# Down-projection of a gated MLP: form before activation at its start, parked transfers one step later, two output rows in its third phase

## The chip, the cores and the metric

The program runs on one core of one Trainium2 chip. The metric is the time of one execution on the device in microseconds (us), the median of several runs. In the profile the engines are PE (TensorE, matmuls), PEld (its weight loads), DVE (VectorE), ACT (ScalarE), POOL (GpSimd) and SP (SyncE, which here only issues DMAs). ACTq and SPq are the instruction queues of ACT and SP; a DMA issued from one stands in it in order with everything else that the engine is given.

## The reference

One layer of a decoder: a conditioned first half (recurrence and sparse attention) and a conditioned gated MLP. The change touches only the second half of the MLP. T = 512 tokens, D = 1024, F = 2816, all f32:

```
h2 = rmsnorm(x, norm2_g) * (1.0 + sc2) + sh2
u = causal_dwconv(h2 @ w_up, conv_w, conv_b)     # 512 x 5632, three taps over the tokens
a, v = split(u, 2, axis=-1)
x = x + gt2 * ((silu(a) * v) @ w_down)           # 512 x 2816 by 2816 x 1024
```

## The kernel before

**Arithmetic.** Each f32 operand is split into a rounded part and a remainder, both in the format fp32r: `split` (L143, L144) casts on ACT (`whi<-raw`) and subtracts on DVE (`wlo<-raw,whi`). Every product is then three matmuls (`mm3`, L147 to L149). In what follows a *form* is such a pair of split weights; `form` puts two of three forms into the buffers `whi`/`wlo` (two of each) and the third into the single buffer `w3`, which the profile shows as `w`. So form k+3 reuses the buffer of form k and its cast has to wait until the matmuls of form k are done.

**Up-projection.** 44 steps `st`, one of 128 columns each; f = st // 2 counts the 22 pairs of gate (s = 0) and value (s = 1). Step st multiplies (`up_mm`, PE tile `u`), and two steps later `up_post` (L1597) makes the convolution of it: an ACT operation (L1603), two on DVE (L1604, L1605), then Silu on ACT for a gate (L1608), and for a value the product with the gate (L1610).

**Down-projection.** It is one level of a seven-product scheme of 2 by 2 blocks: tokens in halves of 256, columns of `w_down` in halves of 512, rows of `w_down` by even and odd f. With two values f of a pair j at hand, `g_parts` (L1627) makes the sums of activations that the seven products need (`s12`, `s34`) and splits them (`gP`, `gQ`, `st22`, `st34`). These are small jobs in a list `work`; each `up_post` starts with `step(3)` (L1621), which issues the next three. The last job of a pair is `park` (L1653): two DMAs on ACT's queue that write `st22` and `st34` to HBM (`pk`), from which they come back later as `S` and `A`.

The products are walked in phases of twelve steps, and a step is one form against the stationary activations of one or two pairs j: 12 matmuls of 512 columns for two pairs, 6 for one. `ORDERS` gives the steps (q, e), q = 0 to 5 a group of weight rows, e one of the phase's two products. The first phase does products 1 and 5 (from `gP`), the second 6 and 2 (from `gQ`), the third 7 and 3 (from `S`), and a last stage does product 4 (from `A`). The weights arrive in four sets, `da`, `db`, `dx` and `dy`, six loads each. In `forms` (L1681) DVE makes weight sums (`sum_a` L1667, `sum_b` L1673 and L1674, `sum_c` L1678) and then the form. `look()` takes the next form from it, three steps ahead.

**Order around the change.** `phase` (L1792) does for each step: the product; if the group q is new, `each(q)`; after step (5, 0) `done()`, which combines accumulators; then `look()`. In the first phase `each(0)` is `up_post` of the last value column, so the last activation work stands ahead of the form for step 3 on ACT and DVE. The gate before it, st = 42, is finished by `up_post` before the phase, with its Silu.

The accumulators are four pairs of PSUM banks (PE and DVE tile `dn`): `bS` is complete after the second phase (first two row tiles, first half of the columns), `bV` after the third (first two row tiles, second half), `bW` after `end_c` near the end of the third phase (last two row tiles, second half), and `bR` at the very end. `dn_out` (L1738 to L1743) multiplies by the gate row `gt2`, adds the residual (`rest`, 512 KB for each row tile, loaded by `load_rest` from `x1d`) and issues the DMA out on SP. In the last stage the loop at L1849 does four steps, each followed by one `dn_out` (`bV[0]`, `bV[1]`, `bW[0]`, `bW[1]`), then L1861 and L1862 scale `bR` and add the residual, and three closing pieces (512, 256 and 256 columns) are multiplied, added on DVE (L1867) and sent out on SP (L1868).

**Queues.** All loads stand in SP's queue in the order in which the program issues them. A load waits there until its tile's buffer is free, and each DMA, of SP or of ACT, takes the next of eight completion semaphores and waits until the DMA that used it eight places before has landed. One that waits holds up all that stands behind it.

Of the kernel before, what the change touches and what calls it, by code (L numbers as in the profile page):

```python
# [102 lines left out]
def hybrid_layer_kernel(ctx: ExitStack, tc: tile.TileContext, d: dict, out: bass.AP, dbg=None):  # L103
# [526 lines left out]
    def each(f):  # L630
        while True:
            f()
            yield
# [960 lines left out]
            mm3(us[st][:, sl], hi[:, k], lo[:, k], h2T[k // 2][0][:, k % 2, sl], h2T[k // 2][1][:, k % 2, sl], k == 0,  # L1594
                k == KT - 1)

    def up_post(st):  # L1597
        f, s = divmod(st, 2)
        u = us.pop(st)
        step(3)  # L1600
        c = s * NFF + f
        y = TMP([P, T], tag="y")
        sc.activation(y, u, AF.Identity, bias=cv[:, 132 + c:133 + c], scale=cv[:, 88 + c:89 + c])  # L1603
        ve.scalar_tensor_tensor(y[:, 1:], u[:, :T - 1], cv[:, 44 + c:45 + c], y[:, 1:], ALU.mult, ALU.add)  # L1604
        ve.scalar_tensor_tensor(y[:, 2:], u[:, :T - 2], cv[:, c:c + 1], y[:, 2:], ALU.mult, ALU.add)  # L1605
        ys[s] = y
        if s == 0:
            sc.activation(y, y, AF.Silu)  # L1608
        else:
            ve.tensor_tensor(ys[0], ys[0], y, ALU.mult)  # L1610
            g_parts(f, ys[0])

# [14 lines left out]
    def g_parts(f, y):  # L1627

        j, odd = divmod(f, 2)
        tt = ve.tensor_tensor  # L1630
        if not odd:
            gP[j] = G([2, 2, 256], F32R, s="gP")
            s4 = G([4, 256], s="s4")
            work.extend([(split, gP[j][:, 0, 0], gP[j][:, 0, 1], y[:, h1]),
                         (tt, s4[:, 2], y[:, h1], y[:, h2], ALU.subtract)])
            evens[0] = y, s4
            return
        e, s4 = evens.pop(0)
        s12, s34 = s4[:, 0:2], s4[:, 2:4]
        gQ[j] = G([2, 2, 256], F32R, s="gQ")  # L1640
        st22 = TMP([P, 2, 256], F32R, tag="st22")
        st34 = G([2, 2, 256], F32R, s="st34")
        work.extend([(tt, s12[:, 0], e[:, h2], y[:, h2], ALU.add),
                     (tt, s12[:, 1], s12[:, 0], e[:, h1], ALU.subtract),
                     (tt, s34[:, 1], y[:, h1], s12[:, 1], ALU.subtract),
                     (split, gQ[j][:, 0, 0], gQ[j][:, 0, 1], y[:, h1]),
                     (split, st22[:, 0], st22[:, 1], y[:, h2]),
                     (split, gP[j][:, 1, 0], gP[j][:, 1, 1], s12[:, 0]),
                     (split, gQ[j][:, 1, 0], gQ[j][:, 1, 1], s12[:, 1]),
                     (split, st34[:, 0], st34[:, 1], s34),  # L1650
                     (park, j, st22, st34)])

    def park(j, st22, st34):  # L1653
# [63 lines left out]
    def product(bank, n, q, w, start=False, rows=False):  # L1717

        hi, lo = w
        bs = range(min(2, NJ - 2 * q))  # L1720
        for a, b in [(a, b) for a in range(2) for b in bs] if rows else [(a, b) for b in bs for a in range(2)]:
            mm3(bank[a], *stat(n, 2 * q + b, a), hi[:, b], lo[:, b], start and q + b == 0, False)
# [63 lines left out]


    look()
    up_post(nst - 2)
    bR, bW, bS, bV = ([PS("dn") for _ in range(2)] for _ in range(4))  # L1790

    def phase(n, xb, x, yb, y, done, each):  # L1792
        seen = set()
        for q, e in ORDERS[n > 0]:
            w = ready.pop(0)
            product((xb, yb)[e], (x, y)[e], q, w, n == 0)
            if q not in seen:
                seen.add(q)
                each(q)
            if (q, e) == (NQ - 1, 0):  # L1800
                if n < 2:
                    sums_first()
                done()
            look()

    def end_a():
        for a in range(2):
# [7 lines left out]
        for a in range(2):  # L1815
            ve.tensor_tensor(bW[a], bR[a], w5[a], ALU.add)

    def each_a(q):
        if q == 0:
            up_post(nst - 1)  # L1820
        else:
            step(3)
            load_s34(q - 1)

    def each_b(q):
        load_s34(q + NQ - 1)

    def gate(q):
        ve.tensor_tensor(keep[q], keep[q], gt2[:, 0:512].unsqueeze(1).to_broadcast(list(keep[q].shape)), ALU.mult)

    def each_c(q):
        if q in (1, 2):
            load_rest()
        if q in (2, 3):
            gate(q + 2)
        if q in (3, 4):
            dn_out(bS[q - 3], q - 3, 0)
        load_a22(q)

    phase(0, bR, 1, bW, 5, end_a, each_a)  # L1840
    w5 = [TMP([P, T], tag="w5") for _ in range(2)]
# [1 line left out]
        sc.copy(w5[a], bW[a])  # L1843
    phase(1, bR, 6, bS, 2, end_b, each_b)
    phase(2, bR, 7, bV, 3, end_c, each_c)
    outs = [(bV[0], 0, 1), (bV[1], 1, 1), (bW[0], 2, 1), (bW[1], 3, 1)]
    lead = slice(0, 512)
    ws = []
    for q in range(NQ):  # L1849
        w = ready.pop(0)  # L1850
        if q < 2:
            load_rest()
        if q < NQ - 2:
            product(bR, 4, q, w, rows=q == NQ - 3)
            look()
            dn_out(*outs[q])
        else:
            ws += [(hi[:, b], lo[:, b], 2 * q + b) for hi, lo in [w] for b in range(min(2, NJ - 2 * q))]
    for a in range(2):
# [3 lines left out]
    for bank, a, cols in ((bS[0], 0, lead), (bS[1], 1, slice(0, 256)), (bV[0], 1, slice(256, 512))):  # L1863
        for n, (hi, lo, j) in enumerate(ws):
            mm3(bank[:, cols], *stat(4, j, a), hi[:, cols], lo[:, cols], n == 0, n == len(ws) - 1)
        t = rest[2 + a][:, cols]
        ve.tensor_tensor(t, bank[:, cols], t, ALU.add)  # L1867
        sp.dma_start(out_view[:, 2 + a, cols], t)  # L1868


_INS = ["x", "c", "positions", "w_ada", "b_ada", "norm1_g", "w_in", "lb_logits", "hg_norm_g", "q_norm_g",
# [18 lines left out]
```

## Time and profile before

| | |
|---|---|
| median of 3 runs | 691.7 us (691.69 to 692.68) |
| the profiled execution | 691.81 us, of which the span from first to last instruction is 690.0 us |
| mean granted TensorE clock | 0.997 |
| PE, DVE, ACT busy | 98%, 81%, 52% of the span |
| up-projection ends, first phase begins | 574.5 us |
| second phase, third phase, last stage begin | 610.0, 639.9, 669.9 us |
| last matmul starts | 684.90 us |

Rows of the timeline give start, duration, engine, line, operation, tiles written and read, and in brackets how long the engine had idled and what released it. A matmul's duration overlaps the next matmul, so the distance between two starts says what one costs. Rows of windows give the window and its length, then busy time (and count) of PE, PEld, DVE, ACT and POOL, the granted PE clock, the share of the 16 DMA engines and GB/s.

### The profile page before, as it was taken

To read this page: it belongs to the slowest core of one execution; us is meant where nothing else is said; L and a number is where in the kernel's file an instruction comes from. 1 tells how busy PE (TensorE), PEld (TensorE's weight loads), DVE (VectorE), ACT (ScalarE), POOL (GpSimd) and SP (SyncE) were. 2 spreads that over 40 slices of the span, in tenths; PEclk is the share of its full clock that TensorE was granted. 3 is DMA by queue.
4 is the path that set the end of the run, shared out by engine and by line. 5 is a ranking of instruction groups with operands and counts; after the bars stand their busy time and mean duration, and the time that the engine had idled before them with its cause. 6 is when DMAs were issued, how large, how long until landed. Compare 5 with 4: busy or idle time off the path is not lost.

```text
span 690.0 us, 10199 instructions
## 1 busy us (share of the span) xinstructions
PE 675.7 (98%) x3749; PEld 560.1 (81%) x3749; DVE 558.9 (81%) x1080; ACT 357.9 (52%) x688; POOL 56.3 (8%) x69
## 2 busy tenths in 40 slices
PE   8999999999999999999999999999999998999997
PEld 4678898687988889888988888888888886888886
DVE  5698988999889898687767787787878777888886
ACT  5564447565577669344554445444545445453431
POOL 1007153403000000200100000000000000000000
PEclk9999999999999999999999999999999999999999
DMA  9996544486123133443353745636634455869943
GB/s 280 291 313 204 151 154 152 142 256 184 32 93 123 32 95 123 151 135 119 119 153 91 200 135 171 185 104 192 197 115 115 120 183 177 298 226 374 367 138 122
DMA packets 107447, 117.48 MB, mean 170 GB/s; under 512 B 6731, under 2 KB 84355, under 8 KB 107397
## 3 DMA queue, kind: packets, MB, share of 16 engines
q1 hardware_dynamic: 103397, 105.98, 49.5%
q10 hardware_dynamic: 4000, 10.86, 4.1%
q8 instruction: 29, 0.48, 0.3%
q14 instruction: 21, 0.17, 0.1%
HBM read 103.96 MB, written 12.85 MB: 169 GB/s over the span
## 4 chain that ended last, share of the span: by engine, by line
PE 74%; DVE 14%; DMA 4%; SPq 3%; ACT 2%; issue 2%; ACTq 0%; POOL 0%; DVEq 0%; POOLq 0%
PE u L147 11%; PE u L148 11%; PE u L149 11%; PE dn L148 4%; PE dn L149 4%; PE dn L147 4%; PE oT L1068 2%; SPq L300 2%; PE F L1040 2%; PE pT L147 2%; PE pT L149 2%; PE pT L148 2%; DVE wlo L144 2%; PE oh L149 2%; PE oh L147 2%; PE oh L148 2%
## 5 line engine op out<-in xcount | busy, mean ns | idle before, releaser
L144 DVE TENSOR_TENSOR wlo<-raw,whi 128x1024 fp32r<-128x1024 f32 (+1 forms) x58 | 70.0, 1207 | 31.7 <-ACT whi L143 31.4
L147 PE MATMUL u<-h2h,whi 128*128 128x512 f32 (+1 forms) x248 | 93.3, 376 | 0.0
L148 PE MATMUL u<-h2l,whi 128*128 128x512 f32 (+1 forms) x248 | 93.1, 375 | 0.0
L149 PE MATMUL u<-h2h,wlo 128*128 128x512 f32 (+1 forms) x248 | 93.1, 375 | 0.0
L143 ACT CAST whi<-raw 128x1024 fp32r<-128x1024 f32 (+1 forms) x58 | 59.2, 1020 | 50.3 <-PE u L148 28.2
L148 PEld LDWEIGHTS u<-h2l,whi 128*128 128x128 f32 x248 | 46.7, 188 | 8.4
L149 PEld LDWEIGHTS u<-h2h,wlo 128*128 128x128 f32 x248 | 46.7, 188 | 8.4
L147 PEld LDWEIGHTS u<-h2h,whi 128*128 128x128 f32 x248 | 46.7, 188 | 8.3
L147 PE MATMUL u<-h2h,w 128*128 128x512 f32 (+1 forms) x128 | 48.1, 376 | 0.0
L148 PE MATMUL u<-h2l,w 128*128 128x512 f32 (+1 forms) x128 | 48.1, 376 | 0.0
L149 PE MATMUL u<-h2h,w 128*128 128x512 f32 (+1 forms) x128 | 48.1, 376 | 0.0
L1008 ACT ACTIVATE pt<-pt,mx 128x128 f32<-128x128 f32 (+3 forms) x64 | 35.8, 561 | 20.7 <-DVE mx L992 20.4
L1603 ACT ACTIVATE y<-u,cv 128x512 f32<-128x512 f32 x44 | 34.1, 775 | 19.4 <-DVE st L144 19.4
L1608 ACT ACTIVATE y<-y 128x512 f32<-128x512 f32 x22 | 13.9, 633 | 56.6 <-DVE y L1605 56.5
L1604 DVE SCALAR_TENSOR_TENSOR y<-u,cv,y 128x511 f32<-128x511 f32 x44 | 32.8, 745 | 12.2 <-ACT y L1603 12.2
L147 PE MATMUL pT<-hT,whi 128*128 128x512 f32 x96 | 38.7, 403 | 0.0
L149 PE MATMUL pT<-hT,wlo 128*128 128x512 f32 x96 | 37.6, 392 | 0.0
L148 PE MATMUL pT<-hT,whi 128*128 128x512 f32 x96 | 37.5, 391 | 0.0
L1605 DVE SCALAR_TENSOR_TENSOR y<-u,cv,y 128x510 f32<-128x510 f32 x44 | 32.9, 748 | 1.5
L1047 ACT COPY pT<-F 128x512 f32<-128x512 f32 (+2 forms) x52 | 25.8, 498 | 12.8 <-PE F L1040 12.4
L992 DVE CUSTOM_DVE_ANT_0 pt<-S,cmask 128x128 f32<-128x128 f32 (+3 forms) x64 | 29.6, 482 | 3.1 <-PE S L987 3.1
L376 POOL TENSOR_TENSOR hrs<-hrs,mhalf 128x4 f32<-128x4 f32 (+2 forms) x16 | 20.2, 1269 | 136.8 <-DVE hrs L375 136.7
(411 smaller groups left out, 1751.0 us busy)
## 6 DMA issues: line engine op xcount, KB each, us to landing
raw<-in_w_up SPq DMA_DIRECT2D x44, 512.0 KB, 5.1
ada<-in_w_ada SPq DMA_DIRECT2D x48, 256.0 KB, 5.2
aw<-in_w_ada SPq DMA_DIRECT2D x24, 512.0 KB, 4.5
raw<-in_w_down SPq DMA_DIRECT2D x10, 1024.0 KB, 4.8
raw<-in_w_in SPq DMA_DIRECT2D x7, 1024.0 KB, 6.2
rawd<-in_w_down SPq DMA_DIRECT2D x12, 512.0 KB, 9.2
pk<-st ACTq DMA_DIRECT2D x11, 512.0 KB, 2.6
S<-pk SPq DMA_DIRECT2D x11, 512.0 KB, 8.3
```

The costliest lines, as they stand in the source:

```text
L143: sc.copy(hi, src)
L144: (eng or ve).tensor_tensor(lo, src, f32(hi), ALU.subtract)
L147: pe.matmul(o, ah, bh, start=start, stop=False, skip_group_check=True)
L148: pe.matmul(o, ah, bl, start=False, stop=False, skip_group_check=True)
L149: pe.matmul(o, al, bh, start=False, stop=stop, skip_group_check=True)
L376: gp.tensor_tensor(o, o, mhalf[:, 0:n], ALU.pow)
L992: ve.tensor_tensor_reduce(pt[:, sl], ps[:, sl], cmask[:, 512 - W:512], -1.0, 1e30, ALU.add, ALU.min, mx[:, e:e + 1])
L1008: sc.activation(pt[:, sl], pt[:, sl], AF.Exp, bias=mx[:, e:e + 1], scale=-1.0, accum_out=su[:, h % 2, e:e + 1])
L1047: sc.copy(pT, ps[:, 0:n * P])
L1603: sc.activation(y, u, AF.Identity, bias=cv[:, 132 + c:133 + c], scale=cv[:, 88 + c:89 + c])
L1604: ve.scalar_tensor_tensor(y[:, 1:], u[:, :T - 1], cv[:, 44 + c:45 + c], y[:, 1:], ALU.mult, ALU.add)
L1605: ve.scalar_tensor_tensor(y[:, 2:], u[:, :T - 2], cv[:, c:c + 1], y[:, 2:], ALU.mult, ALU.add)
```

## The change

It has four parts, all around the down-projection.

1. **`phase` and its callbacks.** A step is now product, `done()`, `look()`, and then `each(k)` with the number of the step. In the first phase `up_post(42)` no longer issues the Silu of the last gate; that stands behind the form for step 3 (`each_a(0)`), and `up_post(43)` stands behind the form for step 4 (`each_a(1)`). The other `step(3)` calls and the loads of `S` move to odd and even steps.
2. **Parking.** An empty job is put ahead of `park`, which so becomes the first job of the next `step(3)`, one `up_post` later.
3. **Third phase.** All four `load_rest` stand in its first four steps, before it was two there and two in the last stage. The outputs of `bS` stand one step earlier, and those of `bW` after its last two steps instead of in the last stage. The last stage keeps the outputs of `bV`.
4. **The second closing piece** goes out on ACT's queue instead of SP's.

No arithmetic is added or removed. The diff:

```
-    def up_post(st):
+    def up_post(st, silu=True):
...
-        if s == 0:
+        if s == 0 and silu:
             sc.activation(y, y, AF.Silu)
-        else:
+        if s:
             ve.tensor_tensor(ys[0], ys[0], y, ALU.mult)
             g_parts(f, ys[0])
...
                      (split, st34[:, 0], st34[:, 1], s34),
+                     (lambda: None,),
                      (park, j, st22, st34)])
...
-    up_post(nst - 2)
+    up_post(nst - 2, False)
...
     def phase(n, xb, x, yb, y, done, each):
-        seen = set()
-        for q, e in ORDERS[n > 0]:
-            w = ready.pop(0)
-            product((xb, yb)[e], (x, y)[e], q, w, n == 0)
-            if q not in seen:
-                seen.add(q)
-                each(q)
+        for k, (q, e) in enumerate(ORDERS[n > 0]):
+            product((xb, yb)[e], (x, y)[e], q, ready.pop(0), n == 0)
             if (q, e) == (NQ - 1, 0):
...
                 done()
             look()
+            each(k)
...
-    def each_a(q):
-        if q == 0:
+    def each_a(k):
+        if k == 0:
+            sc.activation(ys[0], ys[0], AF.Silu)
+        elif k == 1:
             up_post(nst - 1)
+        elif k % 2:
+            step(3)
         else:
-            step(3)
-            load_s34(q - 1)
+            load_s34(k // 2 - 1)
-    def each_b(q):
-        load_s34(q + NQ - 1)
+    def each_b(k):
+        if k % 2:
+            load_s34(k // 2 + NQ - 1)
...
-    def each_c(q):
-        if q in (1, 2):
+    def each_c(k):
+        if k in (0, 1, 2, 3):
             load_rest()
-        if q in (2, 3):
-            gate(q + 2)
-        if q in (3, 4):
-            dn_out(bS[q - 3], q - 3, 0)
-        load_a22(q)
+        if k in (4, 6):
+            gate(k // 2 + 2)
+        if k in (5, 7):
+            dn_out(bS[k // 2 - 2], k // 2 - 2, 0)
+        if k % 2 == 0:
+            load_a22(k // 2)
+        if k > 9:
+            dn_out(bW[k - 10], k - 8, 1)
...
-    outs = [(bV[0], 0, 1), (bV[1], 1, 1), (bW[0], 2, 1), (bW[1], 3, 1)]
...
-        if q < 2:
-            load_rest()
         if q < NQ - 2:
             product(bR, 4, q, w, rows=q == NQ - 3)
             look()
-            dn_out(*outs[q])
+            if q < 2:
+                dn_out(bV[q], q, 1)
...
-        sp.dma_start(out_view[:, 2 + a, cols], t)
+        (sc if cols.start == 0 and a else sp).dma_start(out_view[:, 2 + a, cols], t)
```

**Place one, the start of the first phase, on ACT.** Numbers in the names tell buffers apart: `u_5703` is the last gate column, `u_5744` the last value column, `keep_5788` holds the weight sum for step 3 and `raw_5786` the weights for step 4. Before:

```order
L143 CAST st_1002_5702<-s_991_5621 128x512
L1654 DMA pk_3608<-st_1001_5701 128x512
L1655 DMA pk_3607<-st_1002_5702 128x1024
L1603 ACTIVATE y_5799<-u_5703,cv 128x512
L1608 ACTIVATE y_5799<-y_5799 128x512
L143 CAST gP_5784<-y_5739 128x256
L1603 ACTIVATE y_5827<-u_5744,cv 128x512
L143 CAST whi_5835<-keep_5788 128x1024
L143 CAST whi_5855<-raw_5786 128x1024
```

Now:

```order
L143 CAST st_1002_5702<-s_991_5621 128x512
L1603 ACTIVATE y_5797<-u_5703,cv 128x512
L143 CAST whi_5821<-keep_5788 128x1024
L1817 ACTIVATE y_5797<-y_5797 128x512
L143 CAST whi_5842<-raw_5786 128x1024
L1655 DMA pk_3608<-st_1001_5701 128x512
L1656 DMA pk_3607<-st_1002_5702 128x1024
L143 CAST gP_5784<-y_5739 128x256
L1603 ACTIVATE y_5851<-u_5744,cv 128x512
```

The two parking DMAs stood ahead of the last gate's operation and now stand five rows further on; the casts for steps 3 and 4 stood last and now stand ahead of the small split `gP` and the last value's operation.

**The same place on DVE**, from the last gate's first convolution operation to the second weight sum after it. Before:

```order
L1604 SCALAR_TENSOR_TENSOR y_5799<-u_5703,cv,y_5799 128x511
L1605 SCALAR_TENSOR_TENSOR y_5799<-u_5703,cv,y_5799 128x510
L144 TENSOR_TENSOR gP_5784<-y_5739,gP_5784 128x256
L1625 TENSOR_TENSOR s_1014_5785<-y_5739 128x256
L1604 SCALAR_TENSOR_TENSOR y_5827<-u_5744,cv,y_5827 128x511
L1605 SCALAR_TENSOR_TENSOR y_5827<-u_5744,cv,y_5827 128x510
L1610 TENSOR_TENSOR y_5799<-y_5799,y_5827 128x512
L144 TENSOR_TENSOR wlo_5836<-keep_5788,whi_5835 128x1024
L1667 TENSOR_TENSOR keep_5853<-raw_5786 128x1024
L144 TENSOR_TENSOR wlo_5856<-raw_5786,whi_5855 128x1024
```

Now:

```order
L1604 SCALAR_TENSOR_TENSOR y_5797<-u_5703,cv,y_5797 128x511
L1605 SCALAR_TENSOR_TENSOR y_5797<-u_5703,cv,y_5797 128x510
L144 TENSOR_TENSOR wlo_5822<-keep_5788,whi_5821 128x1024
L1668 TENSOR_TENSOR keep_5840<-raw_5786 128x1024
L144 TENSOR_TENSOR wlo_5843<-raw_5786,whi_5842 128x1024
L144 TENSOR_TENSOR gP_5784<-y_5739,gP_5784 128x256
L1625 TENSOR_TENSOR s_1014_5785<-y_5739 128x256
L1604 SCALAR_TENSOR_TENSOR y_5851<-u_5744,cv,y_5851 128x511
L1605 SCALAR_TENSOR_TENSOR y_5851<-u_5744,cv,y_5851 128x510
L1610 TENSOR_TENSOR y_5797<-y_5797,y_5851 128x512
L144 TENSOR_TENSOR w_1037_5871<-keep_5840,w_1037_5871 128x1024
```

The subtraction for step 3 came eighth and now comes third; that for step 4 passes the same five small operations.

**Place two, the end of the third phase and the last stage, on DVE**, from the split for step 1 of the last stage to the first `L1861`. Before:

```order
L144 TENSOR_TENSOR wlo_6480<-keep_5788,whi_6479 128x1024
L144 TENSOR_TENSOR w_1138_6489<-keep_5853,w_1138_6489 128x1024
L144 TENSOR_TENSOR wlo_6507<-keep_5893,whi_6506 128x1024
L1741 TENSOR_TENSOR tmp_6510<-dn_5810,gt_3609 128x512
L1742 TENSOR_TENSOR tmp_6510<-tmp_6510,rest_6327 128x512
L144 TENSOR_TENSOR wlo_6529<-keep_5937,whi_6528 128x1024
L1741 TENSOR_TENSOR tmp_6532<-dn_5811,gt_3609 128x512
L1742 TENSOR_TENSOR tmp_6532<-tmp_6532,rest_6367 128x512
L144 TENSOR_TENSOR w_1147_6548<-keep_5941,w_1147_6548 128x512
L1741 TENSOR_TENSOR tmp_6551<-dn_5806,gt_3609 128x512
L1742 TENSOR_TENSOR tmp_6551<-tmp_6551,rest_6492 128x512
L1741 TENSOR_TENSOR tmp_6567<-dn_5807,gt_3609 128x512
```

Now:

```order
L144 TENSOR_TENSOR wlo_6482<-keep_5788,whi_6481 128x1024
L1742 TENSOR_TENSOR tmp_6487<-dn_5803,gt_3609 128x512
L1743 TENSOR_TENSOR tmp_6487<-tmp_6487,rest_6334 128x512
L144 TENSOR_TENSOR w_1141_6497<-keep_5840,w_1141_6497 128x1024
L1742 TENSOR_TENSOR tmp_6500<-dn_5804,gt_3609 128x512
L1743 TENSOR_TENSOR tmp_6500<-tmp_6500,rest_6359 128x512
L144 TENSOR_TENSOR wlo_6517<-keep_5890,whi_6516 128x1024
L1742 TENSOR_TENSOR tmp_6520<-dn_5807,gt_3609 128x512
L1743 TENSOR_TENSOR tmp_6520<-tmp_6520,rest_6292 128x512
L144 TENSOR_TENSOR wlo_6537<-keep_5931,whi_6536 128x1024
L1742 TENSOR_TENSOR tmp_6540<-dn_5808,gt_3609 128x512
L1743 TENSOR_TENSOR tmp_6540<-tmp_6540,rest_6317 128x512
```

The four operations on `bW` (`dn_5806` and `dn_5807` before, `dn_5803` and `dn_5804` now) stood behind the last split and now stand ahead of two splits; behind the last split the next operation is now L1863, which was L1861.

**Place three, SP's queue ahead of the weights of steps 9 and 11 of the third phase** (256 KB each: `rawd_6346` and `rawd_6348` before, `rawd_6350` and `rawd_6352` now). Before:

```order
L214 DMA rawd_6268<-in_w_down 128x2x512
L214 DMA rawd_6270<-in_w_down 128x2x512
L1705 DMA A_1105_6288<-pk_3608 128x1024
L214 DMA rawd_6306<-in_w_down 128x2x512
L214 DMA rawd_6308<-in_w_down 128x2x512
L1709 DMA rest_6327<-x1d 128x1024
L1705 DMA A_1113_6329<-pk_3608 128x1024
L214 DMA rawd_6346<-in_w_down 128x512
L214 DMA rawd_6348<-in_w_down 128x512
```

Now:

```order
L214 DMA rawd_6268<-in_w_down 128x2x512
L1701 DMA S_1104_6274<-pk_3607 128x1024
L1710 DMA rest_6292<-x1d 128x1024
L1706 DMA A_1108_6294<-pk_3608 128x1024
L214 DMA rawd_6308<-in_w_down 128x2x512
L214 DMA rawd_6310<-in_w_down 128x2x512
L1710 DMA rest_6317<-x1d 128x1024
L1710 DMA rest_6334<-x1d 128x1024
L1706 DMA A_1116_6336<-pk_3608 128x1024
L214 DMA rawd_6350<-in_w_down 128x512
L214 DMA rawd_6352<-in_w_down 128x512
```

One load of `S` and two of `rest`, 512 KB each, now stand ahead of these weights that stood elsewhere before.

## The prediction

> **What bounds the kernel now.** I read the page's first part, then the waits of PE from 540 us on (the end of the up-projection and all that follows), then PE's timeline there.
>
> ```profile
> span 690.0 us, 10199 instructions
> PE 675.7 (98%) x3749; PEld 560.1 (81%) x3749; DVE 558.9 (81%) x1080; ACT 357.9 (52%) x688; POOL 56.3 (8%) x69
> ```
>
> ```profile
> PE dn L148 <- DVE wlo L144: 2.0, 1, 2.0
> PE dn L147 <- ACT whi L143: 1.4, 1, 1.4
> ```
>
> PE sets the time, and in the last 150 us it waits only twice. The timeline puts both waits into the fourth and fifth step of the first phase:
>
> ```profile
> 577.19 0.39 PE L147 MATMUL dn<-whi,gP 128*128 128x512 f32 x1
> ...
> 579.91 0.39 PE L147 MATMUL dn<-w,gP 128*128 128x512 f32 x1
> ...
> 582.40 0.39 PE L149 MATMUL dn<-w,gP 128*128 128x512 f32 x1
> 584.16 0.50 PE L147 MATMUL dn<-whi,gP 128*128 128x512 f32 x1 [1.37 <-ACT whi L143]
> ...
> 586.65 0.50 PE L148 MATMUL dn<-wlo,gP 128*128 128x512 f32 x1 [1.99 <-DVE wlo L144]
> ...
> 590.63 0.39 PE L149 MATMUL dn<-whi,gP 128*128 128x512 f32 x1
> ```
>
> ```profile
> 582.79:584.16 1.37, 0.00 (x1) 0.01 (x1) 1.33 (x4) 1.37 (x3) 0.00 (x0) 1.00 0.95 350
> 584.66:586.65 1.99, 0.00 (x0) 0.00 (x0) 1.96 (x4) 0.39 (x1) 0.00 (x0) 1.00 0.41 165
> 587.19:590.60 3.41, 3.41 (x9) 2.64 (x8) 3.34 (x6) 1.05 (x1) 0.00 (x0) 0.50 0.21 36
> ```
>
> One step of 12 matmuls lasts 579.91 - 577.19 = 2.72 us. From 582.40 to 590.63 there are again 12 spacings, and they take 8.23. So the hold-up costs 8.23 - 2.72 = **5.5 us**: the waits 1.4 and 2.0, and about 2.1 because the granted clock is 0.50 in the 3.41 us behind them. In both waits DVE is busy from end to end (1.33 of 1.37, 1.96 of 1.99): DVE's order is what PE waits for.
>
> The second place where PE doesn't set the time is the end:
>
> ```profile
> 684.90 0.28 PE L149 MATMUL dn<-w,A 128*128 128x256 f32 x1
> ```
>
> ```profile
> 681.87 0.69 DVE L1742 TENSOR_TENSOR tmp<-tmp,rest 128x512 f32<-128x512 f32 x1
> ...
> 684.52 0.69 DVE L1862 TENSOR_TENSOR rest<-rest,tmp 128x512 f32<-128x512 f32 x1
> 685.13 1.35 DVE L1867 TENSOR_TENSOR rest<-dn,rest 128x512 f32<-128x512 f32 x3
> ```
>
> ```profile
> L1868 SPq DMA_DIRECT2D out_x<-rest x3: 332/452/734, 685.8 to 687.1; - x3
> ```
>
> DVE works without a gap up to 685.13 + 1.35 = 686.48, though the last matmul starts at 684.90; the last piece is issued at 687.1.
>
> **The change at the turn.** ACT and DVE there, before:
>
> ```profile
> 578.75 0.33 ACTq L1655 DMA_DIRECT2D pk<-st  x1
> 579.12 0.78 ACT L1603 ACTIVATE y<-u,cv 128x512 f32<-128x512 f32 x1 [2.57 <-DVE st L144]
> 581.57 0.63 ACT L1608 ACTIVATE y<-y 128x512 f32<-128x512 f32 x1 [1.66 <-DVE y L1605]
> 583.07 1.03 ACT L143 CAST whi<-keep 128x1024 fp32r<-128x1024 f32 x1
> ```
>
> ```profile
> 578.04 0.68 DVE L144 TENSOR_TENSOR st<-s,st 128x512 fp32r<-128x512 f32 x1
> 579.94 0.75 DVE L1604 SCALAR_TENSOR_TENSOR y<-u,cv,y 128x511 f32<-128x511 f32 x1 [1.22 <-ACT y L1603]
> 580.72 0.75 DVE L1605 SCALAR_TENSOR_TENSOR y<-u,cv,y 128x510 f32<-128x510 f32 x1
> 582.52 0.43 DVE L144 TENSOR_TENSOR gP<-y,gP 128x256 fp32r<-128x256 f32 x1 [1.05 <-ACT gP L143]
> ...
> 585.38 1.22 DVE L144 TENSOR_TENSOR wlo<-keep,whi 128x1024 fp32r<-128x1024 f32 x1
> 586.51 1.22 DVE L1667 TENSOR_TENSOR keep<-raw 128x1024 f32<-128x1024 f32 x1
> 587.65 1.22 DVE L144 TENSOR_TENSOR wlo<-raw,whi 128x1024 fp32r<-128x1024 f32 x1
> ```
>
> Today the parking DMA in ACT's queue waits for `st`, and the last gate's operation (L1603) behind it loses 2.57 us. With parking moved down, L1603 starts as soon as its columns are there, at about 576.5, and DVE takes L1604 behind `st` at 578.7, L1605 at 579.5. The cast for step 3 needs the buffer of step 0, which is done when step 1 starts, at 577.19. How soon a cast follows shows at the start of the last stage:
>
> ```profile
> 669.95 0.39 PE L147 MATMUL dn<-whi,A 128*128 128x512 f32 x1
> ```
>
> ```profile
> 670.15 1.06 ACT L143 CAST w<-keep 128x1024 fp32r<-128x1024 f32 x1 [0.30 <-PE dn L149]
> ```
>
> That is 0.20 later, so here 577.4 to 578.4. DVE then subtracts for step 3 from 580.2 to 581.4; PE needs it with the second matmul (0.23 a matmul) of step 3, which without waits starts at 579.91 + 2.72 = 582.63: at 582.9: 1.5 us in hand. The Silu and the cast for step 4 run on ACT up to about 582.0, `keep` on DVE up to 582.5, the subtraction up to 583.7; PE needs that at 582.63 + 2.72 + 0.23 = 585.6: 1.9 in hand. Then come the five operations that had stood ahead (`gP`, L1625, L1604, L1605, L1610), 583.5 to 586.5 by the rows' starts, and the subtraction for step 5, up to 587.6, which PE needs at 588.3: only **0.65** in hand, the tightest place. Steps 6 to 8 have 1.1 to 1.4. So both waits go and nothing new is late. A wait that ends at zero leaves no cause for the 0.50 clock; I take the whole 5.5, a term of **-5.5 us**.
>
> The Trainium skill, "TensorE: Matmul & The Clock Gate", section "What's actually happening", says that the clock halves only after an idle window of about 3.4 us and that the window runs free. The 3.41 us row agrees in length, but the window ahead of it held matmuls (584.16, 586.65), so it was not all idle. By the rule a small wait that were left at step 5 would cost itself alone; by the row perhaps 2.1 more. The sum has no such wait, so it is the same by both.
>
> **Parking in the up-projection.** PE waits nowhere in the up-projection's last 35 us (the two waits above are all since 540), and from 98% busy over the span little can be had before. The DMAs move behind one more `up_post`; their data is read in the third phase. I take 0, between a loss and a gain of at most the 0.33 of one issue. The cover is PE's unbroken work there; without it, each DMA that waits for `st` costs ACT what it cost here, 2.57.
>
> **The third phase** shifts with PE by 5.5, but gets three loads of 512 KB (one `S`, two `rest`) ahead of the last weights in SP's queue:
>
> ```profile
> 610.00:630.00 20.00, 20.00 (x90) 16.57 (x89) 18.18 (x16) 7.88 (x9) 0.00 (x0) 1.00 0.77 282
> 630.00:650.00 20.00, 20.00 (x89) 16.31 (x88) 16.74 (x18) 9.08 (x10) 0.00 (x0) 1.00 1.04 395
> 654.00:656.00 2.00, 2.00 (x11) 1.65 (x10) 1.64 (x2) 0.93 (x1) 0.00 (x0) 1.00 0.15 55
> ```
>
> ```profile
> 653.38 1.22 DVE L1829 TENSOR_TENSOR keep<-keep,gt 128x1024 f32<-128x1024 f32 x1
> ...
> 656.10 1.82 DVE L1678 TENSOR_TENSOR rawd<-rawd,rawd 128x1024 f32<-128x1024 f32 x2
> 658.51 1.23 DVE L144 TENSOR_TENSOR w<-rawd,w 128x1024 fp32r<-128x1024 f32 x1 [0.59 <-ACT w L143]
> ```
>
> ```profile
> 661.79 0.39 PE L147 MATMUL dn<-w,S 128*128 128x512 f32 x1
> ```
>
> The DMA engines are full from 630 to 650 (395 GB/s) and nearly idle from 654, so the last weights have landed by about 653.7. Three loads are 1.57 MB, at 395 GB/s 4.0 us. After the change the last weights land at 653.7 - 5.5 + 4.0 = 652.2. Behind the landing come the second sum (of the L1678 pair, 1.82 - 1.22 = 0.60) and the split (1.23), and PE needs the result at 661.8 - 5.5 = 656.3: a landing up to 654.5 costs nothing, 2.3 us in hand. DVE itself had the split done at 659.74, 2.05 ahead of PE; one gate operation more (L1829, 1.14 to the next row where DVE goes on) stands ahead of it now: 0.9 in hand. Term: 0, with the ends given by the rivals below.
>
> ```profile
> 669.87 1.23 DVE L144 TENSOR_TENSOR wlo<-keep,whi 128x1024 fp32r<-128x1024 f32 x1 [1.27 <-ACT whi L143]
> ```
>
> Four operations of DVE on `bW` move from the last stage to the end of the third phase. Four such stand from 681.87 to 684.52: 2.65 us. DVE idles 1.27 us ahead of the quoted split (step 1 of the last stage) while it waits for a cast, so the place has room. The split is done at 671.1, the next, for step 2, some 1.2 later; now the first two of the four stand between: 671.1 + 1.3 + 1.2 = 673.6. PE needs it at 669.95 + 2 x 2.72 + 0.23 = 675.6, so 2.0 in hand. Term: 0.
>
> **The end.**
>
> ```profile
> L1867 DVE TENSOR_TENSOR rest<-dn,rest x3: 414/415/684, 685.1 to 686.1; 128x256 f32<-128x256 f32 x2, 128x512 f32<-128x512 f32 x1
> ```
>
> Without these four, DVE would be done with L1862 at 685.21 - 2.65 = 682.6 of today's time, so it waits for PE. The third piece starts when the last matmul is done, 684.90 + 0.28 = 685.2, and lasts 0.41: 685.6, issued at once, where before it was issued at 687.1. Term: **-1.4 us**, with 0.1 off for the hand-over. This holds with the second piece on SP too: it would be issued as the third starts, at about 684.9 at the latest, and hold SP for 0.73 at most (the longest of the three issues), up to 685.6. So I give the move to ACT's queue 0; at most 0.3 of an issue either way.
>
> The Trainium skill, "DMA: Bandwidth & Descriptors", section "Issuing engines are not separate DMA queues", says that starting DMAs from several engines saves only the time in which one sequencer starts them. It speaks against more than this 0.3 from the second queue, and the rows here bear that out.
>
> **Sum.** -5.5 - 1.4 = -6.9. The profiled execution took 691.81 us (span 690.0, 1.8 around it), 0.1 above the median of 691.7. 691.8 - 6.9 = **684.9 us**.
>
> **Rivals.**
> - *Half done at the turn*: DVE becomes the bound. It has 0.65 us in hand at step 5; if the operations of DVE ahead of it come 1 to 2 us later than I have them (each hand-over between DVE and ACT that I set at nothing takes some tenths, and the Silu now stands between two casts), PE waits 0.5 to 1.5 there, perhaps with the clock's 2.1: 684.9 + 0.6 to + 3.6, so 685.5 to 688.5. For it: DVE was busy in both waits. Against: all is summed from rows.
> - *Loads in the third phase come late*: with 2.3 us in hand, a landing 2.8 to 4.8 us later than 652.2 gives 0.5 to 2.5 back: 685.4 to 687.4. For it: the DMA engines are full there, and each load waits in SP's queue for a buffer and for one of eight semaphores. Against: the three loads are already counted at the full 4.0 us.
> - *Slower*: the loads run at 282 GB/s, the rate of 610 to 630, not at 395. Those from 630 to 653.7 (23.7 us, 9.4 MB) and the three more (1.57 MB) are 10.9 MB; from 630 - 5.5 = 624.5 on they take 38.8 us, and the last weights land at 663.3. With 1.83 for sum and split PE gets them at 665.1, not 656.3: a wait of 8.8, and 2.1 of clock. -6.9 + 10.9 = +4.0: 695.8. It turns slower than before when the landing is past 654.5 + 6.9 - 2.1 = 659.3, 7 us later than forecast. Against: from 630 to 650 the rate was 395.
> - *The change doesn't do what it says at the turn*: some other wait (a load of weights, POOL) holds the casts. Then the end alone is won: 690.4. Against: the bracket at 579.12 names `st`, and in both of PE's waits DVE was at work on what now stands behind.
>
> **How the numbers follow.** As forecast, 684.3 to 685.6: 0.65. Late loads 0.17; half done at the turn 0.10; not as it says 0.05; slower 0.03. The range leaves out the last two and the upper end of the first rivals: 684.0 (0.3 each for parking, the closing queue and the rounding of the waits below) to 687.8. About 0.2%, 1.4 us, is what a measurement of this kernel can tell from no change; so same is 690.3 to 693.1 and takes the case at 690.4. Faster 0.92, same 0.05, slower 0.03.
>
> **What would show it.** At the turn: PE has no wait from 574 on, granted clock 1.00 from 582 to 591, ACT's L1603 for the last gate starts before `st` is split, the sixth matmul row above (590.63) stands at about 585.1. Later phases begin 5.5 earlier: 604.5, 634.4, 664.4. In the third phase L1678 shows no wait for a DMA above 1 us and PE none at all. At the end the last L1867 starts at the end of the last matmul, and the last issue stands 0.5 behind its start. Wrong would be any PE wait in steps 5 to 8 of the first phase (DVE as bound), a wait of L1678 for `rawd` that reaches PE (loads), or a span above 686.

## The result and the profile after

| | before | after |
|---|---|---|
| median | 692.19 us (4 runs) | 684.86 us (4 runs, 684.53 to 684.99) |
| profiled execution / its span | 691.81 / 690.0 us | 684.53 / 682.8 us |
| second phase, third phase, last stage begin | 609.94, 639.89, 669.95 | 604.10, 634.16, 664.21 |
| last matmul starts | 684.90 | 679.16 |

The ratio is 0.9888, 95% interval 0.9872 to 0.9904: 7.7 us of 692.2 (6.6 to 8.9); the medians differ by 7.3. The prediction was 684.9 in a range of 684.0 to 687.8.

First the head of the page of the changed kernel:

```profile
span 682.8 us, 10188 instructions
PE 673.2 (99%) x3749; PEld 560.2 (82%) x3749; DVE 557.7 (82%) x1080; ACT 357.3 (52%) x688; POOL 56.4 (8%) x69
```

The view of PE's waits from 540 us on, which had two rows before, is empty now (it lists waits above 0.15 us). Three views of the turn answer to those shown of before. PE's timeline (starts of steps 3 and 4, and the matmul of step 5 that first needs the remainder of the weights) and the window over the stretch that had 0.50 in it:

```profile
582.34 0.39 PE L147 MATMUL dn<-whi,gP 128*128 128x512 f32 x1
...
585.06 0.39 PE L147 MATMUL dn<-whi,gP 128*128 128x512 f32 x1
...
588.00 0.39 PE L148 MATMUL dn<-w,gP 128*128 128x512 f32 x1
```

```profile
582.00:591.00 9.00, 9.00 (x42) 7.44 (x41) 8.86 (x13) 3.42 (x4) 0.00 (x0) 1.00 0.98 371
```

ACT's timeline and DVE's:

```profile
576.16 0.78 ACT L1603 ACTIVATE y<-u,cv 128x512 f32<-128x512 f32 x1
577.10 1.06 ACT L143 CAST whi<-keep 128x1024 fp32r<-128x1024 f32 x1 [0.16 <-PE dn L149]
579.16 0.63 ACT L1817 ACTIVATE y<-y 128x512 f32<-128x512 f32 x1 [1.01 <-DVE y L1605]
...
579.82 0.33 ACTq L1655 DMA_DIRECT2D pk<-st  x1
```

```profile
576.94 0.68 DVE L144 TENSOR_TENSOR st<-s,st 128x512 fp32r<-128x512 f32 x1
...
578.99 1.22 DVE L144 TENSOR_TENSOR wlo<-keep,whi 128x1024 fp32r<-128x1024 f32 x1
...
585.23 1.22 DVE L144 TENSOR_TENSOR w<-keep,w 128x1024 fp32r<-128x1024 f32 x1
```

The step from 582.34 to 585.06 takes 2.72 us like any other, and the clock stays at 1.00. L1603 of the last gate no longer has a bracket: it runs before `st` is split, and the parking DMA comes 3.7 us after it. DVE has the remainder for step 3 done at 580.2 where it was done at 586.6, and that for step 5 at 586.45, 1.55 ahead of its matmul at 588.00.

The end, on PE, DVE and in the grouped row of the closing DMAs on SP (count, then shortest, median and longest issue in ns, then first and last start):

```profile
679.16 0.28 PE L149 MATMUL dn<-w,A 128*128 128x256 f32 x1
```

```profile
679.48 0.42 DVE L1869 TENSOR_TENSOR rest<-dn,rest 128x256 f32<-128x256 f32 x1 [0.65 <-PE dn L149]
```

```profile
L1870 SPq DMA_DIRECT2D out_x<-rest x2: 332/332/332, 678.0 to 679.9; - x2
```

The last DVE operation now waits for the last matmul (0.65), no longer in line behind others, and its DMA starts at 679.9. From the last matmul's start to the end of the span it is 3.64 us, where it was 5.10.

Two places further on matter for what follows. The second phase, where the weights of the last group arrive, on DVE and PE; and the third phase, where three more loads stand ahead of the last weights, in windows and on DVE and PE:

```profile
624.21 0.69 DVE L1674 TENSOR_TENSOR keep<-rawd,keep 128x512 f32<-128x512 f32 x1 [1.29 <-DMA rawd<-in_w_down]
624.82 1.22 DVE L144 TENSOR_TENSOR w<-keep,w 128x1024 fp32r<-128x1024 f32 x1
```

```profile
626.09 0.50 PE L148 MATMUL dn<-w,gQ 128*128 128x512 f32 x1
626.43 0.40 PE L149 MATMUL dn<-w,gQ 128*128 128x512 f32 x1
```

```profile
650.00:652.00 2.00, 2.00 (x11) 1.65 (x10) 2.00 (x3) 0.00 (x0) 0.00 (x0) 1.00 0.93 369
652.00:654.00 2.00, 2.00 (x10) 1.66 (x9) 1.41 (x3) 1.18 (x2) 0.00 (x0) 1.00 0.12 43
```

```profile
651.50 1.82 DVE L1679 TENSOR_TENSOR rawd<-rawd,rawd 128x1024 f32<-128x1024 f32 x2
653.91 1.23 DVE L144 TENSOR_TENSOR w<-rawd,w 128x1024 fp32r<-128x1024 f32 x1 [0.59 <-ACT w L143]
```

```profile
656.28 0.39 PE L148 MATMUL dn<-w,S 128*128 128x512 f32 x1
```

In the second phase the split is done at 626.04 and the matmul that reads it starts at 626.09, in its normal distance from its forerunner; the next one comes 0.34 behind it instead of 0.23. PE hardly waits, but nothing is left in hand, and what DVE waited for is a load. This split is of group 4, and the load holds group 5: `forms` puts the sums of both groups ahead of it, so it stands in DVE's queue behind weights that it doesn't read. In the third phase the stream of loads ends at about 652.1, and the split is ready 1.14 us ahead.

### The profile page after: what moved, and what is told of

Its sections match the earlier page's. It is cut to its first block, busy times and chain, and to the rows that moved or that the text cites. A ratio compares the mean times of both kernels' runs of the same rounds, so it can differ in the third digit from the quotient of the medians.

```text
span 682.8 us, 10188 instructions
## 1 busy us (share of the span) xinstructions
PE 673.2 (99%) x3749; PEld 560.2 (82%) x3749; DVE 557.7 (82%) x1080; ACT 357.3 (52%) x688; POOL 56.4 (8%) x69
## 4 chain that ended last, share of the span: by engine, by line
PE 84%; DVE 10%; DMA 3%; ACT 2%; issue 1%; SPq 0%; POOL 0%; ACTq 0%; DVEq 0%; POOLq 0%
PE u L148 12%; PE u L149 12%; PE u L147 12%; PE dn L148 5%; PE dn L149 5%; PE dn L147 5%; PE oT L1068 3%; PE F L1040 2%; PE pT L147 2%; PE pT L149 2%; PE pT L148 2%; PE oh L149 2%; PE oh L147 2%; PE oh L148 2%; DVE wlo L144 1%; DVE aacc L1317 1%
## 5 line engine op out<-in xcount | busy, mean ns | idle before, releaser
L144 DVE TENSOR_TENSOR w<-raw,w 128x1024 fp32r<-128x1024 f32 x18 | 22.0, 1224 | 15.9 <-ACT w L143 15.9
L1603 ACT ACTIVATE y<-u,cv 128x512 f32<-128x512 f32 x44 | 34.1, 776 | 0.0
```

The lines of the kernel that those rows point to most:

```text
L144: (eng or ve).tensor_tensor(lo, src, f32(hi), ALU.subtract)
```

## Experiments

**Theory A**, the prediction's: PE's hold-up at the turn came from the order of DVE's and ACT's jobs, and parking alone is worth little. **Theory B**: the parking DMA in ACT's queue (the wait of 2.57) was the cause. Four kernels take the change apart.

**b_park**, the kernel before with the later parking alone:

```
                      (split, st34[:, 0], st34[:, 1], s34),
+                     (lambda: None,),
                      (park, j, st22, st34)])
```

> The kernel before with only the parking transfers one up_post later. Theory A (the order of the jobs at the turn is the cause, parking alone is worth little): the wait of 2.57 us of ACT for st goes, DVE gets to the last gate's operations 1.2 us earlier (578.7 instead of 579.94), but the five small operations and the last value column still stand ahead of the form for step 3. PE then waits about 2.2 us instead of 3.4 at steps 3 and 4, and the 0.50 clock behind it may stay: 690.5 if the clock still halves, 688.5 if it doesn't. Theory B (the parking transfer in ACT's queue is the cause, and the order of the forms adds little): nearly all of the 5.5 us goes, 686.5.

Measured: 689.33 us against 692.32 of before in the same session, ratio 0.9961 (0.9946 to 0.9975), runs from 688.1 to 692.3. That is 2.7 us less (1.7 to 3.7). PE's timeline, DVE's, and the window behind the later waits, in the profiled execution, which at 692.29 is the slowest of the eight:

```profile
584.33 0.50 PE L148 MATMUL dn<-wlo,gP 128*128 128x512 f32 x1 [1.88 <-DVE wlo L144]
...
628.86 0.50 PE L147 MATMUL dn<-w,gQ 128*128 128x512 f32 x1 [0.93 <-ACT w L143]
...
630.89 0.50 PE L148 MATMUL dn<-w,gQ 128*128 128x512 f32 x1 [1.53 <-DVE w L144]
```

```profile
626.42 1.23 DVE L1674 TENSOR_TENSOR keep<-raw,keep 128x1024 f32<-128x1024 f32 x1 [2.15 <-DMA raw<-in_w_down]
629.01 0.69 DVE L1674 TENSOR_TENSOR keep<-rawd,keep 128x512 f32<-128x512 f32 x1 [1.36 <-DMA rawd<-in_w_down]
```

```profile
632.00:635.40 3.40, 3.40 (x10) 2.63 (x9) 1.77 (x2) 0.28 (x1) 0.00 (x0) 0.51 1.03 403
```

Theory B is out: with parking alone PE still waits 1.88 us for the same subtraction of DVE. But parking alone isn't worth as little as Theory A says. The total lies where A had it, though not all of it for A's reason. At the turn the first phase takes 32.10 us, 2.2 more than the 29.92 of the changed kernel, as A said for a clock that stays. In the second phase new waits of 0.93 and 1.53 us show up, where DVE waits for loads, this time with the clock at 0.51 behind them: that phase takes 34.61 against 29.95 before. This second place was in nobody's sum. The fastest runs (688.1 and 688.2) leave hardly any room for a loss of 4.7 us there, so it is probably not in every run; only this one has a trace. Why the loads are so late in it was not settled.

**b_turn_park**, the kernel before with the new order at the first phase (parts 1 and 2 of the change), later phases as before:

```
+        new = n == 0
+        for k, (q, e) in enumerate(ORDERS[n > 0]):
+            product((xb, yb)[e], (x, y)[e], q, ready.pop(0), n == 0)
+            if q not in seen and not new:
                 seen.add(q)
                 each(q)
...
             look()
+            if new:
+                each(k)
```

> The kernel before with the new order at the first phase and the later parking, second and third phase and last stage as before. Both theories: the 5.5 us of the turn go and the 1.4 us of the end don't: 686.3. If it comes out below 685.5, the loads and outputs of the third phase cost nothing at the end and my term of 1.4 is wrong; above 687.5, the turn's term is smaller than 5.5.

Measured: 686.77, ratio 0.9917 (0.9905 to 0.9930), that is 5.75 us less (4.85 to 6.6). No PE wait from 540 us on.

**b_tail**, the kernel before with part 3 alone (`new = n == 2` in the same lines, and the new `each_c` and last stage):

> The kernel before with only the third phase and last stage of the changed one (rest loads and outputs earlier; the closing pieces all on SP). My sum: 1.4 us less, 690.3, with the turn's two waits 1.4 and 2.0 as before. Rival (the three loads more delay the last weights of the third phase when nothing else is moved): PE waits there, 691 or more.

Measured: 690.29, ratio 0.9971 (0.9960 to 0.9982), 2.0 us less (1.25 to 2.8). PE's waits from 540 us on, and a window over the turn:

```profile
PE dn L148 <- DVE wlo L144: 2.0, 1, 2.0
PE dn L147 <- ACT whi L143: 1.4, 1, 1.4
PE dn L148 <- DVE w L144: 0.4, 1, 0.4
```

```profile
582.00:592.00 10.00, 6.62 (x29) 4.90 (x28) 8.81 (x14) 6.37 (x10) 0.00 (x0) 1.00 0.52 175
```

The two waits at the turn are those of before to a tenth, and yet the clock behind them is 1.00 in this execution, so the same waits do not always bring the slow clock. The first phase takes 33.89 us here, where it took 35.47 before and takes 29.91 in b_turn_park: the waits cost 4.0 us and the slow clock 1.6. The third wait stands at step 8 of the second phase, the place that has nothing in hand in the changed kernel. From the last matmul (684.62) to the end of the span (688.2) it is 3.58 us, as in the changed kernel; the 1.4 that I expected lies within the interval. The two halves, 5.75 and 2.0, add up to the whole, 7.7.

**a_nopark**, the changed kernel with the `lambda: None` taken out, so that parking stands where it stood:

> The changed kernel with the parking transfers where they were before. By rows of before: DVE's operations behind L1603 of the last gate start 1.2 us later, so the subtraction for step 5 comes 0.65 us late; the others stay in time. Theory A: 685.5 (0.6 back), up to 687.6 if so short a wait also halves the clock. Theory B (parking is the cause of the hold-up): 689 to 690.

Measured: 685.57, ratio 0.9901 (0.9888 to 0.9914); the changed kernel has 0.9888. The difference of 0.7 is within the intervals; the trace decides (the first phase takes 30.73 us, 0.8 more than in the changed kernel). PE's wait, and the rows of ACT and DVE that lead to it:

```profile
PE dn L148 <- DVE w L144: 0.4, 1, 0.4
```

```profile
579.40 0.78 ACT L1603 ACTIVATE y<-u,cv 128x512 f32<-128x512 f32 x1 [2.60 <-DVE st L144]
```

```profile
587.91 1.22 DVE L144 TENSOR_TENSOR w<-keep,w 128x1024 fp32r<-128x1024 f32 x1
```

The wait for `st` is back, the subtraction for step 5 is done at 589.13 and PE waits for it, once. So the later parking keeps step 5 clear; without the new order it removes only part of the hold-up, and with it, it is what leaves room.

**a_sp**, the changed kernel with all closing pieces on SP:

```
-        (sc if cols.start == 0 and a else sp).dma_start(out_view[:, 2 + a, cols], t)
+        sp.dma_start(out_view[:, 2 + a, cols], t)
```

> The changed kernel with the second closing piece on SP's queue as before. My sum gave the move to ACT's queue 0: 684.9, the same within 0.2. Rival (the move is what brings the last issue forward): the last issue stands behind the second one's on SP, 0.5 us later, 685.4.

Measured: 685.06 (684.83 to 685.31), ratio 0.9892 (0.9864 to 0.9920). The last matmul and the closing DMAs on SP:

```profile
679.82 0.28 PE L149 MATMUL dn<-w,A 128*128 128x256 f32 x1
```

```profile
L1870 SPq DMA_DIRECT2D out_x<-rest x3: 332/332/332, 678.7 to 680.6; - x3
```

From the last matmul to the end of the span (683.5) it is 3.68 us, with ACT's queue 3.64. The second piece's issue takes 0.33 and is over before the third piece is ready. The move is worth nothing that can be measured.

The next three kernels add work whose result isn't used, to measure how much is left in hand at three places. **Theory C**, from the trace of the changed kernel: the tight place is step 8 of the second phase, not step 5 of the first.

**a_load1**, one more transfer ahead of the second phase's last weights (in `each_b`; `load_more(n)` copies n row tiles of `x1d`, 512 KB each, to `xl`, a tile in HBM):

```
+        if k == 3:
+            load_more(1)
```

> The changed kernel with one more transfer of 512 KB (HBM to HBM, its result unused) in SP's queue right ahead of the last weights of the second phase. Theory C (from the changed kernel's trace: the form for step 8 of the second phase is ready 0.05 us ahead of its matmul, after DVE waited 1.29 us for these weights, so the place has nothing left in hand): all of the transfer shows, 512 KB at 395 GB/s is 1.3 us: 686.2, and PE waits there for DVE's w. My prediction's picture (the second phase only shifts along and the tight places are step 5 of the first phase and the third phase's loads): 684.9 to 685.2.

Measured: 687.10 (685.35 to 689.85, 9 runs), ratio 0.9934 (0.9909 to 0.9958). PE's wait and the row of DVE behind it:

```profile
PE dn L148 <- DVE w L144: 1.6, 1, 1.6
```

```profile
626.72 0.69 DVE L1674 TENSOR_TENSOR keep<-rawd,keep 128x512 f32<-128x512 f32 x1 [3.07 <-DMA rawd<-in_w_down]
```

DVE's wait for the weights grows from 1.29 to 3.07, by 1.78, and PE waits 1.63 where it waited not at all. Theory C holds: the place has no slack, and one transfer of 512 KB ahead of it costs about 2 us. (I had 1.3 us for it, at 395 GB/s. From 618 to 622 the engines moved 329 GB/s here, at which 512 KB take 1.6; whether it also matters that it runs from HBM to HBM is not shown.)

**a_load3**, three such transfers at the start of the third phase (`load_more(3)` under `if k == 0` in `each_c`):

> The changed kernel with three more transfers of 512 KB (HBM to HBM, result unused) at the start of the third phase, ahead of its last weights. The prediction's sum for this place: 4.0 us more of DMA, the last weights land at about 652.1 + 4.0 = 656.1 instead of 652.1, sum and split take 1.83 more, PE needs the result at 656.3: a wait of about 1.6 us, 686.5, or up to 688.6 with the clock. Rival (there is more room than that, since the loads behind can move): 684.9.

Measured: 686.68 (686.60 to 687.04), ratio 0.9917 (0.9887 to 0.9946).

```profile
PE dn L148 <- DVE w L144: 1.0, 1, 1.0
```

```profile
656.07 0.69 DVE L1679 TENSOR_TENSOR rawd<-rawd,rawd 128x512 f32<-128x512 f32 x1 [2.87 <-DMA rawd<-in_w_down]
```

These are PE's wait and DVE's row. The landing at 656.07 is what the sum of megabytes over 395 GB/s gave (656.1), and PE waits for it as the prediction's chain of sum and split says, 1.0 us instead of the 1.6 expected, since PE came to this place 0.5 us later than in the changed kernel (its third phase begins at 634.64, there at 634.16). With the change's own three loads the prediction had 2.3 us in hand at this place; three more, at 4.0 us, use that up.

**a_dve6**, six more operations on DVE ahead of the split for step 5 of the first phase:

```
             up_post(nst - 1)
+            t = TMP([P, T])
+            for i in range(6):
+                ve.tensor_tensor(t, gt2[:, 0:512], gt2[:, 0:512], ALU.mult)
```

> The changed kernel with six more operations of 128x512 on DVE (results unused, 0.6 us apart, 3.7 us in all) ahead of the split for step 5 of the first phase. By the changed kernel's trace that split is ready 1.55 us ahead of its matmul (the prediction had 0.65): PE waits 3.7 - 1.55 = 2.1 us: 687.1 if so long a wait leaves the clock at 1.00, about 689 if it halves it as in the kernel before. By the prediction's 0.65 in hand: 3.0, so 687.9 or 690.

Measured: 689.46 (687.94 to 690.26, 10 runs), ratio 0.9952 (0.9931 to 0.9973). The added row of DVE with the next, the matmul that waits, and two windows behind it:

```profile
585.53 4.32 DVE L1822 TENSOR_TENSOR tmp<-gt 128x512 f32<-128x512 f32 x6
589.76 1.22 DVE L144 TENSOR_TENSOR w<-keep,w 128x1024 fp32r<-128x1024 f32 x1
```

```profile
591.04 0.50 PE L148 MATMUL dn<-w,gP 128*128 128x512 f32 x1 [2.57 <-DVE w L144]
```

```profile
591.10:592.50 1.40, 1.40 (x6) 1.16 (x7) 1.40 (x2) 0.27 (x1) 0.00 (x0) 1.00 0.00 0
592.60:596.00 3.40, 3.40 (x10) 2.62 (x9) 3.33 (x6) 1.76 (x3) 0.00 (x0) 0.50 0.49 134
```

The six take 589.76 - 585.53 = 4.23 us, more than I had taken. 4.23 less the 1.55 in hand is 2.7, and the wait is 2.57: the 1.55 is real. The clock falls behind this single wait, but not at once. Of the ten runs nine have a mean clock of 0.996 to 0.998 and 689.15 to 690.26 us; the one at 1.000 took 687.94, near the forecast without the clock (687.1) plus the 0.5 by which the six were longer. Only one of the ten has a trace, so that the clock fell in nine is read from their times and mean clocks.

Last, a way to give the tight place room. **a_s_behind**: the load of `S` that stands just ahead of the second phase's last weights goes behind the weights that follow (in `each_b`):

```
-        if k % 2:
+        if k == 5:
+            load_s34(NQ)
+        if k % 2 and k != 3:
             load_s34(k // 2 + NQ - 1)
```

> The changed kernel with one load of S (512 KB) moved from ahead of the last weights of the second phase to behind the weights that follow them. Theory C (those weights are what the place with 0.05 us in hand waits for, but PE still just doesn't wait): the form for step 8 of the second phase is ready about 1.3 us ahead of its matmul instead of 0.05, and the time stays at 684.9 within 0.3. If the place already costs something in undisturbed runs, up to 0.3 is won. Rival (the S load is needed or the later loads suffer): 685.5 or more, with a wait in the third phase.

Measured: 685.04 (684.51 to 685.13), ratio 0.9892 (0.9873 to 0.9912). DVE's and PE's rows at step 8 of the second phase:

```profile
623.58 0.68 DVE L1674 TENSOR_TENSOR keep<-rawd,keep 128x512 f32<-128x512 f32 x1
624.85 1.23 DVE L144 TENSOR_TENSOR w<-keep,w 128x1024 fp32r<-128x1024 f32 x1 [0.59 <-ACT w L143]
```

```profile
626.82 0.39 PE L148 MATMUL dn<-w,gQ 128*128 128x512 f32 x1
```

DVE doesn't wait for the load any more, and 0.74 us is in hand (not the 1.3 I expected, since the chain is now DVE and ACT themselves). The time doesn't move.

**a_s_behind_load1**, the same with the extra transfer of a_load1 in the freed place:

> The same with the extra transfer of 512 KB of a_load1 in the place of the S load. Theory C: the moved S load pays for it, PE waits at most 0.5 us at step 8 of the second phase (a_load1: 1.63) and the time is 684.9 to 685.4 (a_load1: 687.1), with no run near 689. If the extra transfer disturbs by something other than its place in the queue (writes to HBM, the completion semaphores), 686.5 or more as in a_load1.

Measured: 685.04 (684.28 to 685.35), ratio 0.9893 (0.9876 to 0.9910), no PE wait above 0.15 us. DVE waits for the load as in the changed kernel again (1.29 there):

```profile
625.02 0.69 DVE L1674 TENSOR_TENSOR keep<-rawd,keep 128x512 f32<-128x512 f32 x1 [1.43 <-DMA rawd<-in_w_down]
```

```profile
626.91 0.50 PE L148 MATMUL dn<-w,gQ 128*128 128x512 f32 x1
```

This matmul comes 0.39 us behind its forerunner, and the phase takes 30.22 us where a_s_behind has 29.92. So it is the place in SP's queue that counts, and the moved `S` load pays for the extra transfer but for some 0.3 us.

## Why the prediction was right, step by step

Phase by phase in the two profiled executions, worked out from the starts in the table and the first matmul of the first phase (574.47 before, 574.18 after):

| stretch | before | after | change | predicted |
|---|---|---|---|---|
| up to the first phase | 574.47 | 574.18 | -0.29 | 0 |
| first phase | 35.47 | 29.92 | -5.55 | -5.5 |
| second phase | 29.95 | 30.06 | +0.11 | 0 |
| third phase | 30.06 | 30.05 | -0.01 | 0 |
| last stage up to the last matmul | 14.95 | 14.95 | 0 | 0 |
| last matmul to the end of the span | 5.10 | 3.64 | -1.46 | -1.4 |

The -0.29 ahead of the first phase lies within the spread of the traces: the nine kernels with the later parking begin that phase between 573.90 and 575.00, the three without it between 574.47 and 575.08.

- *The turn, -5.5.* Right in size and in mechanism: the order of DVE's and ACT's jobs, as b_park (order as before, PE still waits) and b_turn_park (-5.75) show. The parts of the term were mis-sized, which its sum doesn't show because it was read from starts: the prediction has 3.4 for the waits and 2.1 for the clock, but half speed over 3.41 us can take only 1.7, and b_tail, with the same waits and full clock, shows 4.0 and 1.6. A wait costs PE more than its bracket says (0.41 cost 0.8 in a_nopark, 1.88 cost 2.2 in b_park), because the bracket counts from the end of a matmul that the next one would have overlapped, and the matmul behind it comes late too. The clock's part was also less firm than the prediction had it. The 46 runs of the kernel before in the experiments' sessions bear that out: three, with a mean clock of 0.999, took 689.9 to 690.3 us, the 19 at 0.997 a median of 691.96. At full clock the first phase takes 33.89 us with neither part of the change (b_tail), 32.10 with parking alone, 30.73 with the order alone and 29.92 with both, so the order is the larger cause and parking the smaller.
- *Parking, 0.* Right as to the up-projection, incomplete as to the turn. I left a head start out of the margin at step 5: 0.65 forecast, 1.55 found. The parking of the pair ahead had held ACT up too (in before, L1603 at 556.34 waits 1.77 us for `st`); that wait is gone as well, and DVE comes to the turn earlier: it splits `st` 2.76 us behind the start of the first phase (576.94) where before it was 3.57 (578.04). a_nopark, without the later parking, splits it 3.59 behind that start and PE waits 0.41 there; by the prediction's rival "half done at the turn" that is its lower end (685.5), and it comes out at 685.57.
- *The third phase, 0.* Right, with the landing (652.2 forecast, about 652.1 found) and with DVE's 0.9 in hand (1.14 found). a_load3 shows that the reckoning also holds beyond the point where it starts to cost. The rival "slower", by loads at 282 GB/s, didn't happen: the row at 650 to 652 still has 369.
- *The end, -1.4.* Right (-1.46; b_tail has it alone), and ACT's queue is worth nothing (a_sp).
- *What the steps didn't see.* The prediction called step 5 of the first phase the tightest place and made no sum for the second phase. The tightest place is step 8 of the second phase, with 0.05 us: b_tail waits 0.4 there, b_park 0.93 and 1.53 in that phase, a_load1 1.63. In the changed kernel it costs the 0.11 of the table and no more, and as far as the prediction goes that is luck. Had the loads come half a microsecond later, the time would have been off by as much, and no rival named this place.

As to the clock, the Trainium skill ("TensorE: Matmul & The Clock Gate", section "What's actually happening") has it halve after an idle window of about 3.4 us that runs free. The length agrees: in the clock records of the traces the stretch at half speed lasts 3.413 us in before, in b_park and in a_dve6. That the window runs free agrees too: the full-clock stretch ahead of it lasts 580.27, 624.64 and 587.09 us in these three, which is 170, 183 and 172 times 3.413, whatever PE did in between. So in these traces the clock changes only at the ends of windows, and one can lay the windows over PE's waits:

| run | window, us | PE idle in it | clock behind it |
|---|---|---|---|
| before, end of the first wait and second wait | 583.78 to 587.19 | 2.37 | 0.50 |
| a_dve6 | 589.17 to 592.59 | 1.87 | 0.50 |
| b_park, second phase | 628.53 to 631.94 | 1.86 | 0.50 |
| b_tail, first wait and start of the second | 582.13 to 585.54 | 1.65 | 1.00 |
| b_tail, rest of the second wait | 585.54 to 588.95 | 1.74 | 1.00 |
| b_park, turn | 580.74 to 584.15 | 1.70 | 1.00 |
| a_load1 | 626.38 to 629.79 | 1.63 | 1.00 |

That the window must be idle does not agree: somewhat over half of it was enough. This also tells the same two waits of before and b_tail apart: in before the second lay whole in one window, with the end of the first; in b_tail a window's end cut it.

## What to carry to other kernels

Where an engine's queue holds both what the critical engine needs next and jobs that are due later, a table of when each result is ready and when it is read says how much a reordering is worth, to a tenth here. That table must be made for every place at which a load or a form arrives, not only where the change is: the slack that one fix uses up is often somewhere else, and here it was in a phase that the change hardly touches. A wait that is removed also removes what the clock took behind it, but that part comes and goes from run to run, so it is best kept apart in the sum; and what a wait costs is read from the starts on both sides of it, since its bracket says too little.

## What the hardware showed that was not expected

- Waits of PE far below 3.4 us can halve its clock for 3.4 us, and need not: 1.4 and 2.0 us close together did in the profiled execution of before and didn't in that of b_tail. What decides in these traces is how much of one window of 3.413 us is idle: 1.86 us or more was followed by half clock, 1.70 or less was not. At 1.74 both occur: full clock in b_tail, and half clock near the start of the changed kernel's own profile (the window from 11.09 to 14.50). After waits of 0.41 (a_nopark) all four runs had a mean clock of 1.000.
- The granted clock fell after the wait was over, not in it: in a_dve6 the wait ends at 591.04, and the slow stretch begins at 592.59, at the end of a window.
- A mean clock below 1 need not have cost anything: b_turn_park's profiled execution has 0.998, and its clock falls only at 682.1, behind the last matmul.
- One transfer of 512 KB ahead of a load made DVE's wait for that load 1.78 us longer (a_load1), where the 395 GB/s of another stretch would give 1.3.
